# Where the weights' split buffers and everything behind them begin in on-chip memory: a one-core hybrid decoder layer

## The chip, the core and the metric

The kernel runs on one core of one Trainium2 chip. The metric is the device time of one execution in microseconds, the median of the runs shown; shorter is better. The core has a matrix engine (TensorE, PE in the profile, with its weight loads as PEld), a vector engine (DVE), an activation engine (ACT), GpSimd (POOL) and a queue engine (SP), and 128 partitions of on-chip memory on which all of them work. An address here is the byte offset within a partition; every partition has the same layout.

## The reference

One layer of a decoder over 512 tokens of 1024 channels, in float32: a half-step SwiGLU feed-forward block, a mixer in which half of the channels go through a gated linear recurrence and the other half through eight heads of stick-breaking attention, and a second half-step feed-forward block.

```
x = x + 0.5 * swiglu(rms_norm(x, ffn1_norm), ffn1_w_gate, ffn1_w_up, ffn1_w_down)   # 1024 -> 2816 -> 1024
h = rms_norm(x, mix_norm)
xr, gate, q, k, v = split(h @ w_in)                 # 512 columns each
y_rnn = rg_lru_group(xr, gate, ...)                 # conv of 4, gates, recurrence over 512 steps
y_att = stick_breaking(norm(q) * scale, norm(k), v) # 8 heads of 64
x = x + concat(norm(y_rnn), norm(y_att)) @ w_out
x = x + 0.5 * swiglu(rms_norm(x, ffn2_norm), ffn2_w_gate, ffn2_w_up, ffn2_w_down)
```

## The kernel before

The activations are held transposed: eight tiles x0 to x7 of 128 channels by 512 tokens. The matrix engine works in a float32 form of less precision (fp32r), so each operand is split into a high part (a cast to fp32r) and a low part (what the cast left), and each product is three matmuls: high by high, high by low, low by high. `mm3` (L142 to L145) issues these three. Each matmul takes a stationary operand of 128 by 128, which a weight load brings in, and streams a moving operand of up to 512 columns past it.

The weights come from memory in tiles of 4 KB a partition, go into a ring of three raw buffers (`wr`), are cast by ACT into a ring of four high buffers (`wh`) and subtracted by DVE into a ring of four low buffers (`wl`): `weights` (L126) and `parts` (L131). For most of the feed-forward block (`fast`, `matrix`, `product`, L340 to L460) the kernel multiplies 2 by 2 blocks with seven products instead of eight. There `get` (L367) splits the sums of weight blocks into the same rings `wh` and `wl`, and `product` issues the matmuls at L397. A "wide" matrix has, for each of its seven products and four blocks, one matmul of 512 columns and one of 256; a "narrow" one has three of 256. Of the eight pairs done so in a feed-forward block the gate matrix is always wide and the up matrix twice: ten wide and six narrow matrices, which makes 10 x 28 = 280 matmuls of 512 columns and 280 + 6 x 84 = 784 of 256; for both blocks 560 and 1568.

In the feed-forward blocks, the recurrent projections and the output projection the weights are stationary and the activations (`xh`, `xl`, `hh`, `hl`, `xb`, `yrh`, `yah` and so on) are moving. In the projections of q, k and v (`project_qkv`) it is the other way round: the activations' parts are stationary, and the weights' parts in `wh` and `wl` are the moving operand. The first six products of the first feed-forward block (L529 to L590, tiles `first_r`, `first_h`, `first_l` in a pool of their own) run while their weights come in, in an order of their own: for each block of 128 rows six matmuls high by high, six high by low, six low by high.

The tiles are laid out by pools, one behind the other: constants, then `wpool` with the rings `wr`, `wh`, `wl`, then `xpool` with x0 to x7 and the parts of the normed activations, then `stat`, and behind these the pools of each stage. Tiles begin at multiples of 32 bytes. Tile x0 is wider than the others: the 66 columns of gains, biases and other vectors that the kernel needs lie behind its 512 columns and come in the same transfer, 80 columns with 14 columns of zeros.

```
C_RN, C_AN, C_QN, C_KN = 56, 60, 64, 65
NVEC = 80
x0 = xpool.tile([P, T + NVEC], F32, tag="x0", name="x0")
```

A scheduler orders the instructions of each engine when the program is built. All input transfers but one are issued from SP's queue.

Of the kernel before, what the change touches and what calls it, by code (L numbers as in the profile page):

```python
# [9 lines left out]
F32R = mybir.dt.float32r  # L10
# [5 lines left out]
P = 128  # L16
# [30 lines left out]
C_G1, C_GM, C_G2 = 0, 8, 16  # L47
C_CW, C_CB, C_BA, C_BX, C_LAM = 24, 40, 44, 48, 52
C_RN, C_AN, C_QN, C_KN = 56, 60, 64, 65
NVEC = 80  # L50


@with_exitstack
def hybrid_layer_kernel(
# [18 lines left out]
    wpool = ctx.enter_context(tc.tile_pool(name="wpool", bufs=3))  # L73
# [15 lines left out]
    def f32(ap):  # L89
        return ap.bitcast(F32)  # L90

    def bank(name, tag="b"):
        return banks["pool"].tile([P, T], F32, tag=tag, name=name, bufs=banks["tags"][tag])
# [26 lines left out]

    x0 = xpool.tile([P, T + NVEC], F32, tag="x0", name="x0")
    vec = x0[:, T:]
# [3 lines left out]
    def weights(src, name, n=KD * P, rows=1):  # L126
        raw = wpool.tile([P, n], F32, tag="wr", name=f"r_{name}")
        nc.sync.dma_start(raw if rows == 1 else raw.rearrange("p (k m) -> p k m", k=rows), src)
        return parts(raw, name, n)

    def parts(raw, name, n):  # L131
        hi = wpool.tile([P, n], F32R, tag="wh", name=f"h_{name}", bufs=4)
        nc.scalar.copy(hi, raw)  # L133
        lo = wpool.tile([P, n], F32R, tag="wl", name=f"l_{name}", bufs=4)
        nc.vector.tensor_sub(lo, raw, f32(hi))  # L135
        return hi, lo

# [83 lines left out]
    def ffn(name, xn, wg, wu, wd, first, done):  # L221
# [30 lines left out]
        with tc.tile_pool(name=f"ffn_{name}", bufs=1, reuse_waits="tile") as fp:  # L252

            def flat(ap):
                return ap.rearrange("p c t -> p (c t)")
# [89 lines left out]
            def matrix(w, c, p, wide):  # L345


                n = f"{c}{name}{p}"
                q = 4 * P
                raw = fp.tile([P, 4, q], F32, tag="raw", name=f"r{n}", bufs=3)  # L350
                nc.sync.dma_start(raw, w[p].rearrange("p (s w) -> p s w", s=4))
                sums = fp.tile([P, 3, q], F32, tag="sums", name=f"s{n}", bufs=2)
                with tc.issue_after(plain.last.ins):
                    nc.vector.tensor_add(sums[:, 1, :], raw[:, 2, :], raw[:, 0, :])
                s1 = raw[:, 0, :]
                nc.vector.tensor_add(s1, s1, raw[:, 1, :])
                nc.vector.tensor_add(sums[:, 0, :], raw[:, 2, :], s1)
                nc.vector.tensor_add(sums[:, 2, :], raw[:, 3, :], sums[:, 0, :])
                groups = [
                    [raw[:, 2:4, :]],  # L360
                    [sums[:, 0:1, :], raw[:, 0:1, :]],
                    [sums[:, 1:3, :]],
                    [raw[:, 1:2, :]],
                ]
                ws = []

                def get(group):  # L367
                    if group < len(ws):
                        return ws[group]
                    width = sum(a.shape[1] for a in groups[group]) * q  # L370
                    hi = wpool.tile([P, width], F32R, tag="wh", name=f"h_{n}{group}", bufs=4)
                    lo = wpool.tile([P, width], F32R, tag="wl", name=f"l_{n}{group}", bufs=4)
                    o = 0
                    for a in groups[group]:
                        a = flat(a)
                        to = slice(o, o + a.shape[1])
                        nc.scalar.copy(hi[:, to], a)  # L377
                        nc.vector.tensor_sub(lo[:, to], a, f32(hi[:, to]))
                        o += a.shape[1]
                    ws.append((hi, lo))  # L380
                    return hi, lo

                px, py = (bank(f"p{i}{n}", "b")[:, : T if wide else TH] for i in "xy")

                def product(pt, group, half, b, start):
                    wh, wl = get(group)

                    order = [(k, i) for k in range(KD // 2) for i in range(3)]
                    if wide:
                        order = [(k, i) for i in (3, 2) for k in range(KD // 2)]  # L390
                    for k, i in order:
                        s = slice((half * 4 + k) * P, (half * 4 + k + 1) * P)
                        both = held[k, b]
                        l, r = (
                            (wh, both[:, 0, :]), (wh, both[:, 1, :]), (wl, both[:, 0, :]), (wh, flat(both))
                        )[i]
                        nc.tensor.matmul(  # L397
                            pt[:, : r.shape[1]], l[:, s], r, start=start and (k, i) == order[0],
                            stop=(k, i) == order[-1], skip_group_check=True,
                        )  # L400

                return [
                    (px, 0, 0, B11, True), (py, 0, 1, B21, True),
                    (px, 1, 0, T2, False), (py, 1, 1, T1, True),
                    (px, 2, 0, T3, False), (py, 2, 1, B22, False),
                    (px, 3, 0, T4, False),
                ], product
# [124 lines left out]
    def first_products():  # L532

        with tc.tile_pool(name="first", bufs=1, reuse_waits="tile") as fi:
# [8 lines left out]
            for kk in range(KD // 2):  # L543
                s = slice(2 * kk * P, (2 * kk + 2) * P)
                c = 2 * kk * T + NVEC
                if kk == 0:
                    nc.sync.dma_start(x0, xT[:, : T + NVEC])
                else:
# [562 lines left out]
def _layout(x, ffn1_norm, ffn1_w_gate, ffn1_w_up, ffn1_w_down, mix_norm, w_in,  # L1111
            conv_w, conv_b, rg_w_a, rg_b_a, rg_w_x, rg_b_x, rg_lambda,
            q_norm, k_norm, rnn_out_norm, attn_out_norm, w_out,
            ffn2_norm, ffn2_w_gate, ffn2_w_up, ffn2_w_down):
    import numpy as np

    def cols(v):
        return np.asarray(v).reshape(-1, P).T

    def by_block(w):  # L1120

        k, n = w.shape
        return w.reshape(k // P, P, n // P, P).transpose(2, 1, 0, 3).reshape(n // P, P, k)

    def by_pairs(w):


        o = by_block(w).reshape(NF, P, KD, P)
        o = np.concatenate([o[:, :, 0::2], o[:, :, 1::2]], axis=2).reshape(NF, P, KD * P)
        o = np.concatenate([o[1::2], o[0::2]], axis=2)  # L1130
        b = by_block(w)
        o[: PLAIN // 2] = np.concatenate([b[0:PLAIN:2], b[1:PLAIN:2]], axis=2)
        return o

    w = np.asarray(w_in)[0]
    qkv = w[:, 2 * DR :].reshape(KD // 2, 2, P, 3, DR).transpose(3, 0, 2, 1, 4)
    def gates(a, x):

        a, x = np.asarray(a)[0], np.asarray(x)[0]
        o = np.empty((P, NJ, P), a.dtype)  # L1140
        for n in range(2 * NJ):
            r = (n % 2) * HD
            o[r : r + HD, n // 2, r : r + HD] = a[n]
            o[r : r + HD, n // 2, HD - r : 2 * HD - r] = x[n]
        return o.reshape(P, NJ * P)

    def swapped(v):

        return np.asarray(v).reshape(-1, 2, HD)[:, ::-1].reshape(-1)

    vecs = np.concatenate(
        [
            cols(ffn1_norm[0]), cols(mix_norm[0]), cols(ffn2_norm[0]), cols(conv_w[0]),
            cols(conv_b[0]), cols(rg_b_a[0]), cols(swapped(rg_b_x[0])), cols(rg_lambda[0]),
            cols(rnn_out_norm[0]), cols(attn_out_norm[0]),
            cols(np.tile(np.asarray(q_norm[0]), 2)), cols(np.tile(np.asarray(k_norm[0]), 2)),
            np.zeros((P, NVEC - C_KN - 1), np.float32),
        ],
        axis=1,
    )  # L1160

    xt = np.asarray(x)[0].T.reshape(KD, P, T).transpose(1, 0, 2).reshape(P, KD * T)
    a = {
        "xT": np.concatenate([xt[:, :T], vecs, xt[:, T:]], axis=1),
        "w_rg": by_block(w[:, : 2 * DR]),
        "w_qkv": qkv.reshape(3, KD // 2, P, 2 * DR),
        "w_gate": gates(rg_w_a, rg_w_x),
        "w_out": by_block(np.asarray(w_out)[0]),
        "wg1": by_pairs(np.asarray(ffn1_w_gate)[0]),
        "wu1": by_pairs(np.asarray(ffn1_w_up)[0]),  # L1170
        "wd1": by_block(np.asarray(ffn1_w_down)[0]),
        "wg2": by_pairs(np.asarray(ffn2_w_gate)[0]),
        "wu2": by_pairs(np.asarray(ffn2_w_up)[0]),
        "wd2": by_block(np.asarray(ffn2_w_down)[0]),
    }
    return {n: np.ascontiguousarray(a[n]) for n in _INS}
# [21 lines left out]
```

## Time and profile before

| | us |
|---|---|
| median of 2 runs (898.43 to 898.57) | 898.5 |
| the profiled execution | 898.54 |
| its span, first to last instruction | 896.7 |
| PE busy | 891.0 |
| DVE busy | 712.4 |
| ACT busy | 466.2 |
| POOL busy | 72.9 |

The profiled execution lies at the median; 1.8 us of its time lie outside the span. The core's granted TensorE clock was 1.000 of full speed over the span. PE is busy nearly from end to end. Matmuls are pipelined, the ends of PE's rows are modelled, and the durations of neighbouring rows overlap; how fast PE goes is therefore read from the distance between the starts of neighbouring matmuls, called the step below.

### The profile page before, as it was taken

Reading aid. Unit: us, or ns where it says so; the run is one execution under the profiler, and the core shown is the slowest. Engines: PE = TensorE matmul, PEld = TensorE weight load, DVE = VectorE, ACT = ScalarE, POOL = GpSimd, SP = SyncE. Lnnn points to the kernel's source line nnn. Section 1 sums busy time; section 2 is a strip of 40 time slices with the busy share of each in tenths; the row PEclk is TensorE's granted clock in tenths of the full one; section 3 lists DMA queues with packets and bytes.
Section 4 is the critical chain, followed back from the end, with each engine's and each line's share of the span. In section 5 each row is a group of like instructions: output and inputs, shape, how many; then the busy total and the mean of one; then the engine's idle time right before and its main releaser. Section 6 shows DMA issues by size and latency. Waiting matters only on the chain.

```text
span 896.7 us, 12596 instructions
## 1 busy us (share of the span) xinstructions
PE 891.0 (99%) x4880; PEld 757.9 (85%) x4880; DVE 712.4 (79%) x1032; ACT 466.2 (52%) x771; POOL 72.9 (8%) x60
## 2 busy tenths in 40 slices
PE   9999999999999999999999999999999999999998
PEld 7888899888988888877887778888899988998887
DVE  8598789887887669758689959698689977897763
ACT  7255365544654446365768844445256534563450
POOL 0000000000000005544140001400000000000000
PEclk9999999999999999999999999999999999999999
DMA  8324322441233222322132002324322332233302
GB/s 285 110 57 145 116 94 94 133 144 53 95 130 96 75 94 86 115 74 100 63 115 74 26 24 95 114 60 162 118 94 94 117 135 79 94 113 100 89 24 94
DMA packets 27451, 89.19 MB, mean 99 GB/s; under 512 B 2816, under 2 KB 6144, under 8 KB 23296
## 3 DMA queue, kind: packets, MB, share of 16 engines
q1 hardware_dynamic: 27248, 88.26, 29.1%
q8 instruction: 38, 0.62, 0.3%
q14 instruction: 21, 0.17, 0.1%
q10 hardware_dynamic: 144, 0.13, 0.0%
HBM read 86.29 MB, written 2.10 MB: 99 GB/s over the span
## 4 chain that ended last, share of the span: by engine, by line
PE 98%; DVE 1%; DMA 0%; issue 0%; ACT 0%; DVEq 0%
PE pxub L397 5%; PE pxua L397 5%; PE pxga L397 5%; PE pxgb L397 5%; PE pdb L145 5%; PE pdb L143 5%; PE pdb L144 5%; PE pda L145 5%; PE pda L143 5%; PE pda L144 4%; PE pyub L397 4%; PE pyua L397 4%; PE pygb L397 4%; PE pyga L397 4%; PE first_p L580 4%; PE po L143 2%
## 5 line engine op out<-in xcount | busy, mean ns | idle before, releaser
L144 PE MATMUL pdb<-hlb,h_db 128*128 128x512 f32 (+2 forms) x180 | 69.3, 387 | 0.0
L145 PE MATMUL pdb<-hhb,l_db 128*128 128x512 f32 (+2 forms) x180 | 69.2, 388 | 0.0
L143 PE MATMUL pdb<-hhb,h_db 128*128 128x512 f32 (+2 forms) x180 | 68.9, 388 | 0.0
L144 PE MATMUL pda<-hla,h_da 128*128 128x512 f32 x176 | 68.5, 391 | 0.0
L145 PE MATMUL pda<-hha,l_da 128*128 128x512 f32 x176 | 68.3, 392 | 0.0
L143 PE MATMUL pda<-hha,h_da 128*128 128x512 f32 x176 | 67.5, 392 | 0.0
L482 DVE SCALAR_TENSOR_TENSOR x<-pdb,x 128x512 f32<-128x512 f32 (+2 forms) x33 | 21.9, 673 | 33.9 <-PE pdb L145 33.8
L133 ACT CAST h_da<-r_da 128x768 fp32r<-128x768 f32 (+1 forms) x28 | 24.2, 868 | 40.7 <-PE pda L144 15.2
L133 ACT CAST h_db<-r_db 128x768 fp32r<-128x768 f32 (+1 forms) x28 | 24.2, 868 | 39.1 <-PE pdb L144 21.2
L482 DVE SCALAR_TENSOR_TENSOR x<-pda,x 128x512 f32<-128x512 f32 x32 | 21.6, 686 | 22.9 <-PE pda L145 22.8
L145 PEld LDWEIGHTS pdb<-hhb,l_db 128*128 128x128 f32 x180 | 33.8, 188 | 7.0
L144 PEld LDWEIGHTS pdb<-hlb,h_db 128*128 128x128 f32 x180 | 33.8, 188 | 6.5
L145 PEld LDWEIGHTS pda<-hha,l_da 128*128 128x128 f32 x176 | 33.1, 188 | 7.2
L143 PEld LDWEIGHTS pdb<-hhb,h_db 128*128 128x128 f32 x180 | 33.8, 188 | 6.1
L144 PEld LDWEIGHTS pda<-hla,h_da 128*128 128x128 f32 x176 | 33.1, 188 | 6.6
L143 PEld LDWEIGHTS pda<-hha,h_da 128*128 128x128 f32 x176 | 33.0, 188 | 6.3
L173 POOL TENSOR_TENSOR sqa_m<-sqa_m,sq_m 128x512 f32<-128x512 f32 x7 | 11.8, 1685 | 308.4 <-ACT sq_m L172 308.2
L377 ACT CAST h_gb<-rgb 128x512 fp32r<-128x512 f32 (+1 forms) x24 | 18.3, 763 | 23.5 <-PE pdb L144 12.5
L135 DVE TENSOR_TENSOR l_da<-r_da,h_da 128x768 fp32r<-128x768 f32 (+1 forms) x28 | 27.7, 990 | 2.8 <-ACT h_da L133 2.6
L135 DVE TENSOR_TENSOR l_db<-r_db,h_db 128x768 fp32r<-128x768 f32 (+1 forms) x28 | 27.7, 993 | 2.8 <-ACT h_db L133 2.6
L377 ACT CAST h_ua<-rua 128x512 fp32r<-128x512 f32 (+1 forms) x24 | 18.3, 763 | 22.3 <-PE pyga L397 8.7
L377 ACT CAST h_ub<-rub 128x512 fp32r<-128x512 f32 (+1 forms) x24 | 18.3, 763 | 21.8 <-PE pygb L397 8.7
(459 smaller groups left out, 2816.1 us busy)
## 6 DMA issues: line engine op xcount, KB each, us to landing
r_da<-in_wd SPq DMA_DIRECT2D x24, 384.0 KB, 3.1
r_db<-in_wd SPq DMA_DIRECT2D x24, 384.0 KB, 3.1
rga<-in_wg SPq DMA_DIRECT2D x8, 1024.0 KB, 5.9
rua<-in_wu SPq DMA_DIRECT2D x8, 1024.0 KB, 4.8
rgb<-in_wg SPq DMA_DIRECT2D x8, 1024.0 KB, 5.1
rub<-in_wu SPq DMA_DIRECT2D x8, 1024.0 KB, 4.8
r_o<-in_w_out SPq DMA_DIRECT2D x8, 512.0 KB, 3.5
r_gb<-in_wg SPq DMA_DIRECT2D x6, 512.0 KB, 3.6
```

The source lines that it names most:

```text
L133: nc.scalar.copy(hi, raw)
L135: nc.vector.tensor_sub(lo, raw, f32(hi))
L143: nc.tensor.matmul(out_, wh, ah, start=start, stop=False)
L144: nc.tensor.matmul(out_, wh, al, start=False, stop=False)
L145: return nc.tensor.matmul(out_, wl, ah, start=False, stop=stop)
L173: (engine or nc.gpsimd).tensor_add(self.acc, self.acc, sq)
L377: nc.scalar.copy(hi[:, to], a)
L397: nc.tensor.matmul(pt[:, : r.shape[1]], l[:, s], r, start=start and (k, i) == order[0], stop=(k, i) == order[-1], skip_group_check=True,)
L482: nc.vector.scalar_tensor_tensor(x[k][:, t], pt[:, t], 0.5, x[k][:, t], op0=ALU.mult, op1=ALU.add)
L580: nc.tensor.matmul(pts[i], wp[i][:, s], xp[k], start=k == 0 and wp is hi and xp is n1.h, stop=k == KD - 1 and wp is lo,)
```

## The change

The four buffers of the high parts become 96 bytes longer and those of the low parts 32 bytes; the instructions still use the first part of each. The vectors behind x0 become 66 columns, without the 14 columns of zeros. No instruction does more or less than before, apart from the one transfer that brings x0 and its vectors, 578 columns instead of 592.

```diff
-NVEC = 80
+NVEC = 66
...
     def parts(raw, name, n):
-        hi = wpool.tile([P, n], F32R, tag="wh", name=f"h_{name}", bufs=4)
+        hi = wpool.tile([P, n + 24], F32R, tag="wh", name=f"h_{name}", bufs=4)[:, :n]
         nc.scalar.copy(hi, raw)
-        lo = wpool.tile([P, n], F32R, tag="wl", name=f"l_{name}", bufs=4)
+        lo = wpool.tile([P, n + 8], F32R, tag="wl", name=f"l_{name}", bufs=4)[:, :n]
...
-                    hi = wpool.tile([P, width], F32R, tag="wh", name=f"h_{n}{group}", bufs=4)
-                    lo = wpool.tile([P, width], F32R, tag="wl", name=f"l_{n}{group}", bufs=4)
+                    hi = wpool.tile([P, width + 24], F32R, tag="wh", name=f"h_{n}{group}", bufs=4)[:, :width]
+                    lo = wpool.tile([P, width + 8], F32R, tag="wl", name=f"l_{n}{group}", bufs=4)[:, :width]
...
-            np.zeros((P, NVEC - C_KN - 1), np.float32),
```

What it moves is addresses. These are the first bytes of the tiles in the two built programs, and behind each the remainder by 128, which the prediction calls the tile's offset:

```
tile                               before          changed
wr, three raw buffers              19136 ... (64)  the same
wh, buffer 0                       31424 (64)      31424 (64)
wh, buffer 1                       35520 (64)      35616 (32)
wh, buffer 2                       39616 (64)      39808 (0)
wh, buffer 3                       43712 (64)      44000 (96)
wl, buffer 0                       47808 (64)      48192 (64)
wl, buffer 1                       51904 (64)      52320 (96)
wl, buffer 2                       56000 (64)      56448 (0)
wl, buffer 3                       60096 (64)      60576 (32)
x0                                 64192 (64)      64704 (64)
x1 ... x7                          66560 ... (0)   67040 ... (96)
xh, xl (also yrh, yah, ...)        80896 ... (0)   81376 ... (96)
feed-forward pool (hh, hl, xb, raw, sums, ...)
                                   122112 ... (0)  122592 ... (96)
first_r, first_h, first_l          122112 ... (0)  122592 ... (96)
qTh, qTl, kTh, kTl, v              122368 ... (0)  122848 ... (96)
recurrent pool: gel, xc, xch, xcl, nat, ix
                                   185888 ... (32) 186368 ... (0)
```

So before, every activation tile that moves through PE begins at a multiple of 128 bytes and every weight buffer 64 bytes past one; with the change the activation tiles begin 96 bytes past one, and the eight weight buffers stand two at each of the four offsets.

In memory, the rows of the packed x (one row for each partition) become 4162 instead of 4176 floats long, 16648 instead of 16704 bytes.

The order of the instructions stays the same, with one exception on PE, among the first six products (names are the tiles, with the numbers the program gives them; `first_l` is the low part of the weights, `first_p` the sum in which a product is collected):

```order
 L580 MATMUL first_p_135<-xh_a_172,first_l_134 128x512
+L580 MATMUL first_p_139<-xh_a_172,first_l_138 128x512
 L580 MATMUL first_p_119<-xh_a_188,first_h_117 128x512
 L580 MATMUL first_p_123<-xh_a_188,first_h_121 128x512
...
 L580 MATMUL first_p_131<-xh_a_188,first_h_129 128x512
 L580 MATMUL first_p_135<-xh_a_188,first_h_133 128x512
-L580 MATMUL first_p_139<-xh_a_172,first_l_138 128x512
 L580 MATMUL first_p_139<-xh_a_188,first_h_137 128x512
```

The sixth product's matmul with its low weights now stands ahead of five matmuls of the next block instead of behind them; the number of rows on each engine is the same. On SP, the queue of the input transfers, one row changes, the shape of the first transfer:

```order
-L547 DMA x_93<-in_xT 128x592
+L547 DMA x_93<-in_xT 128x578
```

The transfer stays the first of its queue.

## The prediction

> **What bounds the kernel now.** I read the page's busy times and its chain first, then PE's timeline at places that differ in the offsets of the change, then the counts of matmuls by line.
>
> ```profile
> PE 891.0 (99%) x4880; PEld 757.9 (85%) x4880; DVE 712.4 (79%) x1032; ACT 466.2 (52%) x771; POOL 72.9 (8%) x60
> ...
> PE 98%; DVE 1%; DMA 0%; issue 0%; ACT 0%; DVEq 0%
> ```
>
> PE is busy for 99% of the span and is 98% of the chain that ended last. Nothing that another engine gains or loses by a little shows; what counts is PE's step, the distance between the starts of neighbouring matmuls. No instruction is added or removed, so the question is whether the step depends on where the operands lie. The trace of before has three combinations of offsets (a tile's first byte, modulo 128), and I read the step in each from the start column (the first).
>
> The first products, moving operand at offset 0 and weights at 0:
>
> ```profile
> 17.90 1.52 PE L580 MATMUL first_p<-xh_a,first_h 128*128 128x512 f32 x6
> 19.26 1.52 PE L580 MATMUL first_p<-xl_a,first_h 128*128 128x512 f32 x6
> 20.62 1.52 PE L580 MATMUL first_p<-xh_a,first_l 128*128 128x512 f32 x6
> 21.98 1.52 PE L580 MATMUL first_p<-xh_a,first_h 128*128 128x512 f32 x6
> ```
>
> From 17.90 to 21.98 there are 18 matmuls: a step of 226.7 ns. The down product of the feed-forward block, moving operand at 0, weights at 64, three matmuls of `mm3` in turn:
>
> ```profile
> 86.41 0.39 PE L143 MATMUL pda<-hha,h_da 128*128 128x512 f32 x1
> ...
> 88.47 0.39 PE L143 MATMUL pda<-hha,h_da 128*128 128x512 f32 x1
> ```
>
> Nine matmuls lie between these starts: 228.9 ns. The projection of q, where the weights' parts move (offset 64) and the activations (offset 0) are stationary, in the same turn of three:
>
> ```profile
> 385.05 0.39 PE L143 MATMUL pq<-h_q,xh_m 128*128 128x512 f32 x1
> ...
> 387.85 0.39 PE L143 MATMUL pq<-h_q,xh_m 128*128 128x512 f32 x1
> ```
>
> Twelve matmuls: 233.3 ns. So with the same size and turn the step is 4.4 ns longer where the moving operand begins 64 bytes past a multiple of 128, and 6.6 ns longer than in the first products. The matmuls of 256 columns, moving at 0 and weights at 64, stand in the chain in two kinds (start, length, count):
>
> ```profile
> 125.29 1.41 PE pxua L397 x12
> 126.70 1.39 PE pyga L397 x8
> 128.09 1.36 PE pxua L397 x12
> 129.45 1.36 PE pyua L397 x12
> ```
>
> 1.41 us for 12 is 117.5 ns each, 1.36 is 113.3 ns. The row of 8 is four matmuls of 512 and four of 256; at 117.5 for the narrow ones it leaves 230 ns for each wide one. The counts, by line (L143, L144, L145, L397, L580 in this order; the number in brackets):
>
> ```profile
> 0.00:897.00 897.00, 283.34 (x724) 1.00 0.30 99
> 0.00:897.00 897.00, 281.78 (x724) 1.00 0.30 99
> 0.00:897.00 897.00, 282.23 (x724) 1.00 0.30 99
> 0.00:897.00 897.00, 319.65 (x2128) 1.00 0.30 99
> 0.00:897.00 897.00, 33.78 (x144) 1.00 0.30 99
> ```
>
> Of the 3 x 724 = 2172 matmuls of `mm3`, q, k and v have 3 x 4 x 8 x 3 = 288, and the last block has 24 short ones: 1860 remain at offsets 0 and 64. L397 has 560 of 512 columns and 1568 of 256.
>
> **The change part by part.**
>
> *The moving operands leave the multiples of 128* (x, `xh`, `xl`, `hh`, `hl`, `xb`: offset 96). No row shows a full matmul with its moving operand at 96. The nearest is q's: another offset that isn't 0, 6.6 ns over the first products. I take these 6.6 ns for any moving operand that begins off a multiple of 128.
>
> *The weight buffers spread over 64, 32, 0 and 96.* The feed-forward step is 2.2 ns over that of the first products, whose weights stand at 0. I take it as the price of weights off a multiple of 128, and it falls on three buffers of four: 1.7 ns. The new step is then 226.7 + 6.6 + 1.7 = 235.0 ns for 512 columns, and 113.3 + 6.6 + 1.7 = 121.6 ns for 256, where now I set 116, between the two kinds.
> - `mm3`: 1860 x (235.0 - 228.9) = 11.3 us
> - L397, 512 columns: 560 x (235.0 - 230) = 2.8 us
> - L397, 256 columns: 1568 x (121.6 - 116) = 8.8 us
> - first products: 144 x (235.0 - 226.7) = 1.2 us
> - q, k, v: the moving weights stand at 0 in one buffer of four (5.0 instead of 6.6), the stationary activations go off 0 (+2.2): 288 x 0.6 = 0.2 us
>
> Together 24.3 us, all on PE and so on the path. The ends: if 233.3 is the whole step with a moving operand off 0 and the narrow matmuls stay as they are, 1860 x 4.4 + 560 x 3.3 + 144 x 6.6 ns = 11.0 us; if each of the 2420 + 1568 + 144 matmuls pays 6.6 ns on what it has now, 27.3 us. A gain isn't excluded; it is a rival below.
>
> *DVE, ACT and weight loads at other offsets.* Before, the recurrent pool stands at offset 32, and its rows answer to those at 0 (durations minimum/median/maximum in ns, or the mean after the bar):
>
> ```profile
> L748 DVE TENSOR_TENSOR gel<-gel,rb_r x4: 684/684/693, 464.7 to 466.5; 128x512 f32<-128x512 f32 x4
> L750 ACT ACTIVATE yrh<-gel,x x4: 710/714/717, 466.3 to 468.7; 128x512 fp32r<-128x512 f32 x4
> ...
> L317 DVE TENSOR_TENSOR bsb<-bsb,rb_b 128x512 f32<-128x512 f32 x8 | 5.0, 684 | 0.0
> ...
> L157 ACT ACTIVATE xh_m<-x,x 128x512 fp32r<-128x512 f32 x7 | 5.0, 717 | 3.5 <-DVE x L482 3.5
> ```
>
> 684 against 684 ns, 714 against 717: nothing. Were a row to become a few per cent longer, PE's 99% would cover it; DVE's 79% leaves 184 us.
>
> *Transfers.* x0's transfer loses 56 of 2368 bytes a row; at its 3.4 us that is at most 0.1 us. The rows of x now begin at any multiple of 8 bytes in memory.
>
> ```profile
> 0.00:20.00 20.00, 18.79 (x80) 1.00 0.88 279
> ...
> x<-in_xT SPq DMA_DIRECT2D x7, 256.0 KB, 4.4
> ...
> x<-in_xT SPq DMA_DIRECT2D x1, 296.0 KB, 3.4
> ```
>
> In the first 20 us the transfer engines are busy for 88%, so there a loss would show; later they have 0.30 and the raw rings ahead of them. [...] I take 0.3, between 0 and 0.5. [...]
>
> *The one moved matmul* of the first products has the work of five others ahead of or behind it on a PE that is in step there: nothing.
>
> Sum: 24.3 + 0.3 = 24.6 us on the profiled 898.54, which is the median: 923.1 us.
>
> **The rivals.**
>
> *The step has nothing to do with the offsets.* Then 898.8 us. For it: the two kinds of narrow rows, 113.3 and 117.5 ns, stand side by side with the same offsets, so something else moves the step by 4 ns; and q differs from the down product also in what is stationary. And the matmuls of 64 rows, two at a time, of which the gates' move at offset 32 and the attention scores' at 0:
>
> ```profile
> 392.48 0.40 PE L706 MATMUL pa<-xcl,gate_h 64*128 64x512 f32 x2
> ...
> 393.41 0.41 PE L706 MATMUL pa<-xch,gate_l 64*128 64x512 f32 x2
> ...
> 471.01 0.40 PE L942 MATMUL pz<-kTl,qTh 64*128 64x512 f32 x2
> 471.24 0.39 PE L942 MATMUL pz<-kTh,qTl 64*128 64x512 f32 x2
> ```
>
> Four pairs in 0.93 us, 232 ns, against 230. Against it: those pairs have a step of their own at both offsets, which may hide a price; and the three steps of the full matmuls keep to their combination of offsets in every stretch I read. [...]
>
> *Faster.* What costs 2.2 ns in the feed-forward blocks may be that all eight weight buffers stand at the same offset, 64 from the moving operand's; spreading them would end it. If all steps became those of the first products and the faster narrow row: 1860 x 2.2 + 560 x 3.3 + 1568 x 2.7 + 288 x 6.6 ns = 12.1 us, so 886.4 us. Against it: the moving operands leave 0 at the same time, and the only such row is the slowest. To be faster by 18 us the step would have to fall to about 222 ns, which no full matmul here shows.
>
> **How the numbers follow.** The forecast (moving operands off 128 cost what q's cost) 0.57: its own range is 909.5 to 926.5, from the two ends with the transfers, and 0.04 of it may lie above. No dependence 0.27, at 898.8. Faster 0.16. Within 2% (880.6 to 916.5), which is about what a measurement of this kernel can tell from no change, lie the second case, a quarter of the first (0.14) and most of the third (0.10): 0.51. Slower by more: 0.43. Faster by more: 0.06. The range must take in the second case and the first case's ends: 897.5 to 926.5, leaving out the faster case and what lies above.
>
> **What would show it.** In the profile after: the step of the down product about 235 ns instead of 228.9; of the first products 235 instead of 226.7 (they lose the only combination at 0 and 0); rows of twelve narrow matmuls of about 1.46 us; q's step unchanged within 2 ns. DVE's and ACT's rows of 128x512 unchanged at 684 and 717 ns. PE 99% busy as before. The prediction is wrong if the down product's step stays at 229 or falls, or if PE begins to wait for another engine.

## The result, and the profile after

The changed kernel takes 909.1 us (median of two runs, 909.05 to 909.15) against 898.5 us: 1.0118 times the time before, 95% interval 1.0102 to 1.0134. That is 10.6 us more, where 24.6 us were forecast.

The page of the kernel after, busy times and the chain that ended last:

```profile
PE 901.2 (99%) x4880; PEld 761.3 (84%) x4880; DVE 713.2 (79%) x1032; ACT 466.5 (51%) x771; POOL 71.8 (8%) x60
...
PE 98%; DVE 1%; DMA 0%; issue 0%; ACT 0%; DVEq 0%
```

PE's busy time rose by 10.2 us with the same 4880 matmuls and the span by 10.7 us, to 907.4; the granted clock is 1.000 as before. PE waits for nothing new: the time went into the step. The same three places as in the prediction, from PE's timeline of the kernel after (start, length, instruction): the first products, the down product, q.

```profile
18.15 1.52 PE L580 MATMUL first_p<-xh_a,first_h 128*128 128x512 f32 x6
...
22.23 1.07 PE L580 MATMUL first_p<-xh_a,first_h 128*128 128x512 f32 x4
...
90.76 0.39 PE L144 MATMUL pda<-hla,h_da 128*128 128x512 f32 x1
...
97.03 0.39 PE L144 MATMUL pda<-hla,h_da 128*128 128x512 f32 x1
...
388.01 0.40 PE L143 MATMUL pq<-h_q,xh_m 128*128 128x512 f32 x1
...
390.81 0.40 PE L143 MATMUL pq<-h_q,xh_m 128*128 128x512 f32 x1
```

Eighteen matmuls of the first products in 4.08 us are 226.7 ns each, just as before, although weights and moving operand now begin at offset 96 instead of 0. Twenty-seven matmuls of the down product in 6.27 us are 232.2 ns, against 228.9. Twelve of q in 2.80 us are 233.3 ns, as before. The matmuls of 256 columns, from the chain of waits of the kernel after (start, length, count):

```profile
126.70 1.41 PE pxua L397 x12
128.11 1.41 PE pyga L397 x8
129.52 1.42 PE pxua L397 x12
130.94 1.43 PE pyua L397 x12
```

Rows of twelve take 1.41 to 1.43 us, 118 to 119 ns a matmul, where before rows of 1.36 and 1.41 stood mixed. The whole of L397 in one window (PE busy first) is 4.7 us longer than the 319.65 us before:

```profile
0.00:920.00 920.00, 324.35 (x2128) 296.79 (x2128) 1.00 0.29 97
```

DVE and ACT are as they were: groups of the kernel after at the offset 96 (busy time and mean ns behind the bar), 684 and 717 ns before and after.

```profile
L317 DVE TENSOR_TENSOR bsb<-bsb,rb_b 128x512 f32<-128x512 f32 x8 | 5.0, 684 | 0.0
...
L157 ACT ACTIVATE xh_m<-x,x 128x512 fp32r<-128x512 f32 x7 | 5.0, 717 | 3.4 <-DVE x L482 3.4
```

To see where the 10.6 us went, I added up all steps of PE in both traces, by line and shape (each start taken from the next; steps over 245 ns, at waits and short blocks, apart):

| us | before | after | moved by | forecast |
|---|---|---|---|---|
| `mm3` without q, k, v | 424.9 | 430.8 | +5.9 | +11.3 |
| L397, 512 columns | 128.8 | 130.1 | +1.3 | +2.8 |
| L397, 256 columns | 182.1 | 185.5 | +3.4 | +8.8 |
| first products | 31.4 | 31.4 | 0.0 | +1.2 |
| q, k, v | 64.6 | 64.4 | -0.2 | +0.2 |

Together the moves make 10.4 us. (One matmul of 512 columns behind a wait is counted into its line.) The three large terms have between two fifths and a little over half of their forecast, and the first products have none of it: that points at the price itself, not at a count.

### The profile page after: what moved, and what is told of

Its sections match the earlier page's. It is cut to its first block, busy times and chain, and to the rows that moved or that the text cites. A ratio compares the mean times of both kernels' runs of the same rounds, so it can differ in the third digit from the quotient of the medians.

```text
span 907.4 us, 12596 instructions
## 1 busy us (share of the span) xinstructions
PE 901.2 (99%) x4880; PEld 761.3 (84%) x4880; DVE 713.2 (79%) x1032; ACT 466.5 (51%) x771; POOL 71.8 (8%) x60
## 4 chain that ended last, share of the span: by engine, by line
PE 98%; DVE 1%; DMA 0%; issue 0%; ACT 0%; DVEq 0%
PE pxua L397 5%; PE pxub L397 5%; PE pxgb L397 5%; PE pxga L397 5%; PE pdb L143 5%; PE pdb L144 5%; PE pdb L145 5%; PE pda L143 5%; PE pda L145 5%; PE pda L144 5%; PE pyua L397 4%; PE pyub L397 4%; PE pygb L397 4%; PE pyga L397 4%; PE first_p L580 4%; PE po L143 2%
```

## The experiments

Two theories are told apart here. The prediction's: the price is put on each operand's own offset, modulo 128. Its rival: what counts is the **distance**, the first byte of the stationary operand less that of the moving one, modulo 256. By the addresses above it is 192 everywhere in the feed-forward blocks of the kernel before (31424 leaves 192 over multiples of 256, 122112 leaves 0), 64 in q, k and v, where the roles are swapped, and 0 in the first products, in both kernels. (Slices of 128 columns are 512 bytes apart and don't change it. The gates' small matmuls of the recurrent part, whose moving tiles stand at offset 32 before and 0 after, are an exception to this, and to what was said above of all activation tiles.) With the change it is 224, 64, 160 and 0 for the four high buffers, and 96, 128, 160 and 192 for the low ones.

The expectations of the first four runs call the prediction's theory "theory 1" and take the distance modulo 128, without its sign ("theory 2"): they call 0 what is 128 here in w0_m0 and w64_m64, and 32 what is 224 here in vec_only. Their "theory 3" is that neighbouring buffers at different offsets cost, wherever the moving operands are.

All times, with the ratio to the kernel before on the same chip and its 95% interval:

| run | us | ratio |
|---|---|---|
| vec_only | 908.98 | 1.0117 [1.0097, 1.0137] |
| pads_only | 908.71 | 1.0114 [1.0099, 1.0129] |
| w0_m0 | 910.17 | 1.0130 [1.0115, 1.0145] |
| w64_m64 | 910.25 | 1.0131 [1.0116, 1.0146] |
| both_32 | 898.49 | 0.9998 [0.9989, 1.0008] |
| x_256 | 898.63 | 1.0000 [0.9990, 1.0010] |
| x_128 | 904.10 | 1.0058 [1.0043, 1.0073] |
| dist0 | 900.46 | 1.0020 [1.0011, 1.0030] |
| x_32 | 914.36 | 1.0175 [1.0161, 1.0189] |
| first_64 | 899.46 | 1.0010 [1.0000, 1.0019] |
| split_dist | 899.79 | 1.0013 [1.0005, 1.0022] |
| lo_128 | 907.36 | 1.0095 [1.0080, 1.0111] |
| pairs_64 | 906.49 | 1.0088 [1.0074, 1.0102] |
| two_dist | 897.80 | 0.9988 [0.9979, 0.9997] |
| two_dist_dve | 894.93 | 0.9957 [0.9944, 0.9971] |

In the traces PE's 4880 matmuls stand in the same order as before, apart from two rows in vec_only (those of the change) and 19 in two_dist and two_dist_dve.

### The two halves of the change, and equal offsets

vec_only takes the shorter vectors alone, which moves all that lies behind x0 by 32 bytes; pads_only takes the longer buffers alone and moves what lies behind them back to multiples of 256 (for room, two small tiles of the recurrent part, `half_c` and `neg_c`, become one).

```diff
-NVEC = 80
+NVEC = 66
```

pads_only:

```diff
+        hi = wpool.tile([P, n + 24], F32R, tag="wh", name=f"h_{name}", bufs=4)[:, :n]
+        lo = wpool.tile([P, n + 8], F32R, tag="wl", name=f"l_{name}", bufs=4)[:, :n]
...
+    scales = mp.tile([P, 2 * NJ], F32, tag="scales", name="scales", bufs=1)
+    half_c, neg_c = scales[:, :NJ], scales[:, NJ:]
```

> All eight weight buffers at 64 as before the change, the moving operands at 96 as after it. Theory 1: the steps of the changed kernel or a little more, 909 to 912 us. Theory 2: the distance is 32 for every matmul, which in the changed kernel gave 233.2 ns: every feed-forward step at 233, about 911 to 913 us. Theory 3: 898 to 900 us, step 229.

> The eight weight buffers at the four offsets 64, 32, 0, 96 as in the changed kernel, the moving operands back at offset 0. Theory 1 (what costs is the moving operand off a multiple of 128): the down product's step is back at 229 ns and the time at 898 to 900 us. Theory 2 (what counts is the distance between the offsets of the stationary and the moving operand, modulo 128): the distances are spread over 0, 32, 64, 96 exactly as in the changed kernel, so its steps of 231 to 233 ns and about 909 us stay. Theory 3 (what costs is that neighbouring weight buffers stand at different offsets, wherever the moving ones are): also about 909 us.

Measured: 1.0117 and 1.0114. Either half alone costs about what both together cost (10.6, 10.3 and 10.6 us), so the effects don't add; and it costs about the same to move the moving operands alone as to move the weights alone. That the totals agree so well is partly chance, for their parts differ: by the sums of steps `mm3`, narrow and wide matmuls lose 7.5, 1.0 and 1.8 us in vec_only, 5.7, 3.3 and 1.4 in pads_only. pads_only is where theories 2 and 3 had it and not at the 898 to 900 us of theory 1. vec_only lies at the lower end of theory 1 and below the 911 to 913 of theory 2; theory 3 falls with it, since its weight buffers all stand at 64.

w0_m0 puts both operands at multiples of 128, by 64 bytes ahead of the weights and 64 behind x0; w64_m64 leaves the weights at 64 and brings the moving operands there as well, by the second of the two edits alone.

```diff
+    const.tile([P, 16], F32, tag="gap", name="gap")
...
-    x0 = xpool.tile([P, T + NVEC], F32, tag="x0", name="x0")
+    x0 = xpool.tile([P, T + NVEC + 16], F32, tag="x0", name="x0")
```

> Weight buffers and moving operands all at offset 0 (the kernel before with 64 bytes of space ahead of the weights and 64 more behind x0). Theory 1, as the prediction had it: the feed-forward step falls to the 226.7 ns of the first products, 887 to 892 us. Theory 2: the distance is 0 everywhere; the first products (226.7 ns at distance 0, before and after) say the same, the changed kernel's pairs at distance 0 (231.7 ns) say 905 us. Theory 3: 898.5 us, nothing changes.

> Weight buffers and moving operands all at offset 64 (the kernel before with 64 more bytes behind x0). Theory 1: the moving operand is off a multiple of 128, so the step rises to 233 to 235 ns and the time to 908 to 923 us. Theory 2: distance 0 as in the kernel with both at 0, and the same time as that one. Theory 3: 898.5 us.

Measured: 1.0130 and 1.0131, the same time at different offsets. The down product in PE's timeline of w0_m0, 27 matmuls apart:

```profile
90.82 0.39 PE L145 MATMUL pda<-hla,h_da 128*128 128x512 f32 x1
...
97.09 0.39 PE L145 MATMUL pda<-hla,h_da 128*128 128x512 f32 x1
```

232.2 ns. By the prediction's step this is the combination of the first products, both operands at 0 modulo 128, and should have taken 226.7. That theory falls here. In both kernels the distance is 128.

### The distance, varied and held

both_32 moves everything by 32 bytes (a gap of 8 floats ahead of the weights). x_128, x_256 and x_32 move only what lies behind x0, by 128, 256 and 32 bytes (32, 64 and 8 more columns). dist0 has the gap of 16 floats and 48 more columns, which makes the distance 0 for all large products.

both_32, then x_128, then dist0:

```diff
+    const.tile([P, 8], F32, tag="gap", name="gap")
```

```diff
-    x0 = xpool.tile([P, T + NVEC], F32, tag="x0", name="x0")
+    x0 = xpool.tile([P, T + NVEC + 32], F32, tag="x0", name="x0")
```

```diff
+    const.tile([P, 16], F32, tag="gap", name="gap")
...
-    x0 = xpool.tile([P, T + NVEC], F32, tag="x0", name="x0")
+    x0 = xpool.tile([P, T + NVEC + 48], F32, tag="x0", name="x0")
```

> Everything from the constants on begins 32 bytes later: weights at 96, moving operands at 32, their distance as before the change. Theory A (an operand's own offset counts): moving operands and weights leave their places, 908 to 911 us like all four kernels so far. Theory B (only the distance between stationary and moving operand counts): the time of before, 898.5 us, and a down product step of 229.0 ns.

> The kernel before with 256 more bytes behind x0: the distance modulo 256 stays 192, modulo 512 it goes from 192 to 448. If the distance counts modulo 256: 898.5 us and 229.0 ns. If it counts modulo 512 or more: another time, 900 to 911 us.

> The kernel before with 128 more bytes behind x0, so weights stay and the moving operands go 128 bytes on: both keep their offsets modulo 128, the distance modulo 256 goes from 192 to 64. If the distance counts modulo 128: 898.5 us. If it counts modulo 256: q's products had 64 before the change and 233.3 ns, so the feed-forward steps go to 233 ns and the time to 909 to 911 us. If the own offsets modulo 128 count: 898.5 us.

> 64 bytes of space ahead of the weights and 192 more behind x0: the distance is 0 modulo 256 in the feed-forward blocks, as it is in the first products of every kernel so far (226.7 ns in all of them). Theory B with a period of 256: the feed-forward step falls to 226.7 ns, the narrow step to 113.3, the wide one from 230 to 226.7, q, k and v from 233.3 to 226.7: 898.5 less 12, 886 to 888 us. Theory A (own offsets, both 0 modulo 128): 910 us, as with weights and moving operands both at 0 already measured. If the first products owe their step to their order instead: 899 to 911 us.

> The kernel before with 32 more bytes behind x0: the distance is 160 modulo 256 in every feed-forward matmul, and 96 in q, k and v. If the distance alone counts, the step is that of the changed kernel's buffers with this distance (233.2 ns), the time 908 to 911 us. If the changed kernel's price comes from neighbouring buffers with different distances: 229 ns and 898 to 901 us.

Measured: nothing changes when all moves together (both_32: 0.9998, although no operand of the large products is left at a multiple of 64), and nothing when the moving side goes by 256 bytes (x_256: 1.0000). By 128 bytes it changes. So the quantity is a difference, and a shift of it by 256 bytes left the time as it was. The sizes were expected less well: x_128 stays below its 909 to 911 us, x_32 lies above its 908 to 911, and dist0 misses the 886 to 888 us clearly; the table below shows why. Two places in the timelines, first x_128, then dist0, each pair 27 matmuls apart:

```profile
91.32 0.40 PE L144 MATMUL pda<-hla,h_da 128*128 128x512 f32 x1
...
97.62 0.39 PE L144 MATMUL pda<-hla,h_da 128*128 128x512 f32 x1
```

```profile
89.65 0.39 PE L145 MATMUL pda<-hla,h_da 128*128 128x512 f32 x1
...
95.77 0.39 PE L145 MATMUL pda<-hla,h_da 128*128 128x512 f32 x1
```

233.3 ns at distance 64, 226.7 at distance 0, which is the step of the first products in another place, with other operands. The means over all such groups in each trace (three matmuls of `mm3` in turn, q, k and v apart; for L397 the matmuls of the narrow products, and all those of 512 columns), in ns:

| distance | run | `mm3` | L397, 256 columns | L397, 512 columns |
|---|---|---|---|---|
| 0 | dist0 | 227.5 | 119.7 | 231.0 |
| 64 | x_128 | 233.3 | 113.7 | 232.4 |
| 128 | w0_m0, w64_m64 | 232.8 | 118.7 | 232.7 |
| 160 | x_32 | 233.4 | 119.9 | 233.2 |
| 192 | before, both_32, x_256 | 229.1 | 116.3 | 229.9 |
| 224 | vec_only | 233.3 | 116.8 | 233.2 |

The best distance is not the same for all: 0 for `mm3`, 64 for the narrow matmuls, 192 for the wide ones. That is why dist0 is not faster than before: its sums of steps against the kernel before are -2.7 us for `mm3` and -1.9 for q, k, v, but +4.8 for the narrow matmuls and +0.6 for the wide; another 1.3 us more stand in the steps over 245 ns, most of them at q, k and v. In x_128 `mm3` pays 7.5 us and the narrow matmuls gain 3.3. And x_32, the worst, pays 7.8 us in `mm3`, 6.0 in the narrow and 1.8 in the wide ones, which is the 15.8 us measured to 0.2.

Writes and reads of the other engines move with these tiles too. They are not what sets the step: in each of the traces of before, dist0, x_128, x_32, w0_m0 and vec_only 44 to 50 groups of `mm3` run while DVE, ACT and POOL are all idle, and their means are 229.0, 226.8, 233.3, 233.3, 233.2 and 233.3 ns, the same as in the table to 0.7.

first_64 tests the distance where nothing else has changed it: 64 bytes ahead of the first products' own tiles, so that their weights stand 64 from the moving operand.

```diff
+            fi.tile([P, 16], F32, tag="gap", name="gap")
```

> 64 bytes of space ahead of the first products' own tiles and nothing else: their distance modulo 256 goes from 0 to 64. If the distance rules them as it rules the feed-forward blocks: their step goes from 226.7 to 233 ns, 144 x 6.6 ns = 0.9 us, 899.4 us. If they owe 226.7 ns to their order (six matmuls with the same moving operand into six sums): the step stays and so does the time, 898.5 us.

The first products in PE's timeline of first_64:

```profile
18.16 1.56 PE L581 MATMUL first_p<-xh_a,first_h 128*128 128x512 f32 x6
...
22.36 0.86 PE L581 MATMUL first_p<-xh_a,first_h 128*128 128x512 f32 x3
```

Eighteen matmuls in 4.20 us, 233.3 ns instead of 226.7, and 0.9 us for the 144 of them in the whole time (1.0010, an interval that begins at 1.0000). The rest of the trace is as before. So the step follows the distance in these products too, whose matmuls run in another order, six of a kind in a row.

### What mixed distances cost

With the change, a product's three matmuls often have two distances. lo_128 separates that: 128 bytes between the rings of high and low buffers and 128 behind x0, so that the high parts stand at 192 everywhere and the low parts at 64. pairs_64 puts 64 bytes behind every buffer (and merges the two small tiles again), which gives blocks with one distance and blocks with two.

lo_128, then pairs_64:

```diff
+        if not banks.setdefault("gap", False):
+            banks["gap"] = wpool.tile([P, 32], F32, tag="gap", name="gap", bufs=1)
...
+    x0 = xpool.tile([P, T + NVEC + 32], F32, tag="x0", name="x0")
```

```diff
+        hi = wpool.tile([P, n + 16], F32R, tag="wh", name=f"h_{name}", bufs=4)[:, :n]
+        lo = wpool.tile([P, n + 16], F32R, tag="wl", name=f"l_{name}", bufs=4)[:, :n]
```

> 128 bytes of space between the ring of high parts and the ring of low parts, and 128 more behind x0: each matmul with high weights keeps its distance of 192, each with low weights gets 64. If each matmul pays by its own distance, the three-matmul step is the mean of two at 192 and one at 64, (2 x 229.05 + 233.25)/3 = 230.5 ns, and the time about 901 us. If a change of distance between neighbours costs in itself (the changed kernel's and the pads' mixed pairs): 232 ns or more, 904 to 909 us.

> 64 bytes behind each high and each low buffer: the buffers' distances go 192, 0, 64, 128, high and low of one block always alike. If a stretch of matmuls pays by its distance, the three-matmul steps of the four buffers are those of the four kernels with one distance (229.05, 227.5, 233.25, 232.8 ns; narrow 116.2, 119.7, 113.6, 118.7), the mean step 230.7, the time 902 to 904 us. If buffers with different distances in the rings cost in themselves: steps of 232 to 233 ns in all four and 907 to 910 us.

Measured: 1.0095 and 1.0088; lo_128 is where it was expected if changing distances cost in themselves, pairs_64 lies between its two ranges. In lo_128 the mean step of `mm3` is 232.2 ns. Two matmuls in three at the step of 192 and one at that of 64 would make 230.5. So the alternation has a price of its own in most places, but not in all. The timeline of lo_128, in the gate product of the first block and in its down product, 27 matmuls between the rows of each pair:

```profile
56.13 0.40 PE L146 MATMUL pga<-xl_a,h_ga 128*128 128x512 f32 x1
...
62.43 0.40 PE L146 MATMUL pga<-xl_a,h_ga 128*128 128x512 f32 x1
...
90.86 0.39 PE L146 MATMUL pda<-hla,h_da 128*128 128x512 f32 x1
...
97.04 0.39 PE L146 MATMUL pda<-hla,h_da 128*128 128x512 f32 x1
```

233.3 ns in the one and 228.9 in the other, with the same two distances. In x_128, q and k have one distance, 192, and yet from its timeline:

```profile
384.21 0.40 PE L143 MATMUL pq<-h_q,xh_m 128*128 128x512 f32 x1
...
390.51 0.40 PE L143 MATMUL pq<-h_q,xh_m 128*128 128x512 f32 x1
...
431.80 0.39 PE L143 MATMUL pk<-h_k,xh_m 128*128 128x512 f32 x1
...
437.98 0.39 PE L143 MATMUL pk<-h_k,xh_m 128*128 128x512 f32 x1
```

Again 233.3 and 228.9 ns. So a distance doesn't fix the step by itself: at 192 it is 233.3 ns over 27 matmuls of q and 228.9 over 27 of k. (At distance 0, in dist0, four groups of three in five take 226.7 ns.) What picks the step was not found. In pairs_64 high and low of one block are not always alike, as was expected: by the addresses in the built program blocks whose high part stands at 0 have their low part at 128, and the other way round. Blocks with one distance come out close to the table (0: 228.0, 64: 233.0, 128: 232.3, 192: 230.2 ns), and those that mix 0 and 128 at 231.5 (high at 0) and 232.9 (high at 128).

### Giving each product its best distance

split_dist leaves the weights alone and puts 192 bytes ahead of `hh` and `hl` and again ahead of `xb`, in the feed-forward pool.

```diff
+                if p == 0:
+                    fp.tile([P, 48], F32, tag="gap1", name=f"gap1{name}")
...
+                fp.tile([P, 48], F32, tag="gap2", name=f"gap2{name}")
```

> The kernel before with two spaces of 192 bytes within the feed-forward pool: the parts of the down product's activations (hh, hl) come to distance 0, the summed activations (xb) to distance 64, the rest stays at 192. By the steps measured so far (three-matmul products 227 ns at 0 against 229 at 192; narrow matmuls 113.6 at 64 against 116.1; wide ones 232.4 against 230): down product 1056 x 1.6 to 2.3 ns less, about half of the narrow matmuls 2.5 ns less, half of the wide ones 2.4 more: 898.5 less 2.5 to 4, 894.5 to 896 us. If distances don't act by operand but by the whole layout: 898.5 us or more.

Measured: 1.0013, a miss. The down product reaches distance 0 and a mean of 228.0 ns, but in L397 some moving operands now stand at distance 64 and others at 192, one product beside the other, and its matmuls of 256 columns take 184.5 us in all instead of 182.1.

two_dist moves the weights' side instead: dist0's edits, and within buffers 256 bytes longer, `get` writes its sums 64 bytes further in. `mm3` has distance 0, all of L397 has 64. The room comes from the second buffer for the squares of the norms.

```diff
+                sq = stat.tile([P, T], F32, tag="sq", name=f"sq_{n}{j}", bufs=1)
...
+                    hi = wpool.tile([P, width + 64], F32R, tag="wh", name=f"h_{n}{group}", bufs=4)[:, 16 : 16 + width]
+                    lo = wpool.tile([P, width + 64], F32R, tag="wl", name=f"l_{n}{group}", bufs=4)[:, 16 : 16 + width]
```

> All operands at distance 0 for the three-matmul products, and the weights' parts of the seven-product blocks 64 bytes further into the same buffers, so that these have the distance 64 throughout; the buffers become 256 bytes longer to keep the distance alike over the ring, for which the squares of the norms get one buffer instead of two. By the steps of the kernels with one distance: from 900.5 us at distance 0 the 1568 narrow matmuls lose 5.1 ns each and the 560 wide ones gain about 1: 893 us, 0.6% below the kernel before. If the mix of the two within the feed-forward block costs as in the kernel with split distances, or the single square buffer makes PE wait: 898 to 902 us.

Measured: 897.8 us, 0.9988, not the 893 of the first case. The steps are there (`mm3` 227.4 ns, narrow 114.5), but PE has a new wait. The view of waits of two_dist, engine PE (total, times, longest):

```profile
PE pst_b L181 <- POOL sqa_b L174: 1.1, 1, 1.1
```

and its windows around the end of that wait (length, busy times, and behind them the granted clock, the DMA share and GB/s):

```profile
571.00:573.00 2.00, 2.00 (x13) 1.78 (x13) 1.94 (x3) 0.17 (x1) 0.98 (x1) 1.00 0.11 33
573.00:575.00 2.00, 2.00 (x7) 1.57 (x6) 0.09 (x1) 0.00 (x0) 0.96 (x1) 0.52 0.81 285
575.00:577.00 2.00, 2.00 (x7) 1.52 (x7) 0.00 (x0) 0.00 (x0) 0.00 (x0) 0.62 0.57 211
```

With one buffer for the squares, ACT can write the next square only when POOL has added the last one, and PE, which needs the sum for the norm, waits for POOL: 1.1 us. The wait ends at 570.69 us. The granted clock is 1.00 in the window from 571 us and 0.52 and 0.62 in the next two, and eight matmuls, from 573.07 to 576.46 us, take 424 ns each, 1.6 us more than at 227. The eleven runs of two_dist bear this out in part: eight have a granted clock of 0.998 over the span and take 897.7 to 898.5 us, the other three have 1.000 and take 896.4 to 896.8. So the clock did not fall in each run of the same program, and where it fell it cost about 1.3 us. two_dist_dve gives these additions to DVE:

```diff
-                n2.square(x[k], k)
+                n2.square(x[k], k, nc.vector)
```

> The layout of two_dist (three matmuls of mm3 and the first products at distance 0, the sums of L397 at distance 64), with the squares of the second norm of a feed-forward block's end summed on DVE instead of POOL, so that PE doesn't wait for POOL on the single square buffer. If that wait and the lower clock behind it are what kept two_dist at 897.8 us: 894 to 895.5 us, 0.4% below the kernel before, with steps as in two_dist (mm3 227.4 ns, narrow 114.5 ns). If the loss lies in the steps themselves or in waits elsewhere: 897 to 898.5 us.

Measured: 894.93 us, 0.9957 [0.9944, 0.9971], within what was expected if the wait and the clock behind it were the loss; neither the wait nor a lower clock is in its trace. Of the 2.9 us that it gains on two_dist, the clock makes about 1.3 by the figures above, and of the other 1.6 the wait is 1.1. The window from 573 us in its trace (PE busy, granted clock, DMA share, GB/s), the down product in its timeline, and the narrow matmuls in its chain of waits:

```profile
573.00:575.00 2.00, 2.00 (x10) 1.00 0.76 233
```

```profile
89.52 0.39 PE L145 MATMUL pda<-hla,h_da 128*128 128x512 f32 x1
...
95.64 0.39 PE L145 MATMUL pda<-hla,h_da 128*128 128x512 f32 x1
```

```profile
124.60 1.36 PE pxua L398 x12
...
127.35 1.36 PE pxua L398 x12
128.71 1.36 PE pyua L398 x12
```

27 matmuls in 6.12 us, 226.7 ns, and the rows of twelve at 1.36 us, the faster of the two kinds before. Its sums of steps against the kernel before: `mm3` -2.8, q, k, v -1.7, narrow -2.3, wide +1.6, and 1.5 us more in gaps: 3.7 us, which is what the time shows. This layout is faster than the kernel before by 0.4%, and so than the changed kernel.

## Why the prediction was wrong

**What bounds the kernel** held: PE at 99% before and after, nothing but its step moved the time, and adding up steps by line gives the measured difference to 0.2 us.

**The step that failed** is "6.6 ns for any moving operand that begins off a multiple of 128", with its companion, the "price of weights off a multiple of 128". Both are prices on an operand's own address. What the runs showed in their place is the distance between the two operands of a matmul, modulo 256: w0_m0 and w64_m64 take the same time at different offsets, both_32 has no operand left at its old offset and loses nothing, and first_64 makes the first products slow by moving their weights' tiles alone.

The three steps read before fit both explanations: the first products have distance 0, the down product 192 and q 64, and three numbers with three combinations could not choose. Reading q as "the moving operand is off 128" was the wrong half: in w0_m0 q's moving weights and its stationary activations both begin at multiples of 128. From its timeline, 27 matmuls apart:

```profile
382.78 0.39 PE L144 MATMUL pq<-h_q,xh_m 128*128 128x512 f32 x1
...
389.07 0.40 PE L144 MATMUL pq<-h_q,xh_m 128*128 128x512 f32 x1
```

Still 233.0 ns.

That the time rose, as forecast, does not bear out the price: with the same prices both_32 should have been slower too, and w0_m0 faster. The change lost time because it left the distance 192 for distances that are mostly worse, and that the forecast had the right sign is luck as far as its mechanism goes.

Term by term:
- `mm3`, 11.3 us forecast, 5.9 found. The step was to be 235.0 ns. After, groups of three with one distance (160) are at 233.1, near the table's 233.4, and the common mixed ones at 231.7 (high at 64, low at 192), 231.8 (0 and 128) and 233.2 (224 and 96). 233.4 was the highest mean for any single distance; the two prices do not add up: vec_only and pads_only cost 10.6 and 10.3 us, both together 10.6.
- L397, 2.8 and 8.8 us forecast, 1.3 and 3.4 found. The narrow matmuls were given 121.6 ns; 119.9 is the highest mean at any single distance, and the seven distances that the change spreads them over make 118.3.
- First products, 1.2 us forecast (by its own prices 1.3, since all of these weights leave offset 0), nothing found: the distance stayed 0.
- q, k, v: 0.2 forecast, -0.2 found; the two prices it is made of are not there, so that it came out near is chance.
- DVE and ACT: 684 and 717 ns, unchanged, as forecast.
- Transfers, 0.3 us: no run shows this term. Seven transfers of x take 4.5 us at the median from issue to landing, where they took 4.4. The first products' last unbroken stretch in the chain starts at 6.02 us instead of 5.78, but in kernels with the old rows of x it starts anywhere from 4.87 (split_dist) to 7.41 us (x_128).
- The moved matmul: nothing, as forecast; the first products' step around it is 226.7 ns.

**The rivals.** "The step has nothing to do with the offsets" falls with vec_only: 32 bytes cost 10.6 us. The argument that stood there for it (two kinds of narrow rows with the same offsets) was sound for what it says, since one distance has more than one step (113.3 and 117.5 ns for the narrow matmuls at 192), but didn't carry that conclusion. "Faster" had the right quantity, the weights' place as seen from the moving operand's. Its wrong half was to expect the spread to be good: the kernel before stood at 192 throughout its feed-forward blocks, of the six distances measured the second best for `mm3` and for the narrow matmuls and the best for the wide, and the spread leaves it for distances that are mostly worse.

## What to carry to other kernels

On a kernel that PE fills, treat the distance between the stationary and the moving operand, modulo 256 bytes, as something to measure: here it moves the step by up to 3% (means of 227.5 to 233.4 ns for `mm3`; 5% for 256 columns, 113.7 to 119.9) and the whole time from 0.9957 to 1.0175. A tile added or shortened anywhere ahead of the operands can change it (by 32 bytes in vec_only: 1.0117), so one or two per cent after a change that "only" moves memory may be sought there; shifting both sides together (both_32, 0.9998) changed nothing. Before putting a price on one property of three places in a trace, list every property in which the three differ; a run that sets one of them apart costs less than a sum built on the wrong one.

## What the runs showed of the hardware

- In these runs the step of a full fp32r matmul goes with the distance modulo 256 of its operands (226.7 ns at 0 in most groups of dist0; in the mean 233.4 at 160 in x_32 and 233.3 at 224 in vec_only, up to 6.7 ns more), and not with either address by itself (both_32 0.9998, x_256 1.0000). No run shows why the distance matters. Nor does a run tell apart whether the matmul's own stationary operand counts or the next one's, which is loaded while it streams (PEld is busy for 757.9 us beside PE's 891.0 in a span of 896.7): where all operands have one distance the two are the same. Why the best distance differs between 256 and 512 columns stays open too.
- One distance can have two steps, each held over 27 matmuls and more: 228.9 and 233.3 ns for k and q in x_128. What chooses between them is open, and so the table's means hold for this program's order.
- A single wait of PE of 1.1 us in two_dist, which ended at 570.69 us, was followed from 573 us on by a granted clock of 0.52 and 0.62 in two windows and eight steps of 424 ns; without the wait (two_dist_dve) it stayed at 1.00 there. It was seen in one profile; the granted clocks of the runs (0.998 in eight of eleven, 1.000 in three) say that the clock does not fall in every run of that kernel. What else a fall depends on, no run shows.
